# Moving three groups of loads in a hybrid decoder step on one Trainium2 core: y ahead of its tile's products, a block ring of four places, one decode state block per token

## The chip, the cores and the metric

The kernel runs on one core of a Trainium2 chip. A core has TensorE (PE in the profile, its weight loads PEld), VectorE (DVE), ScalarE (ACT), GpSimd (POOL) and SyncE (SP). In this kernel SP issues almost all loads and POOL almost all stores; SPq and POOLq are the queues from which they do so, and a DMA instruction whose buffer isn't free yet holds up everything behind it in its queue. The metric is the device time of one launch in microseconds (us), lower is better. Before the change three runs gave a median of 926.04 us (925.16 to 929.1).

## The reference

One layer of a decoder step with two groups of heads, in fp32, for one prompt of 1024 tokens (width 1024) and for 8 decode sequences of one new token each:

```python
hn = rmsnorm(x, g_norm)
u = hn @ w_in                          # 1024 x (1024 x 8200)
xa, za, uq, uk, uv, uo, zb, ui, uf = jnp.split(u, SPLIT_IDX, axis=-1)
yA, hA, bufA = rglru_branch(xa, ...)   # causal convolution of 4, gates, linear scan
hB, C, n, m = mlstm_seq(q, k, v, ...)  # 4 heads of 256, chunks of 128 tokens
yB = rmsnorm_per_head(sigmoid(uo) * hB) * g_mhead
merged = concatenate([yA * silu(za), yB * silu(zb)])
x = x + merged @ w_out                 # (1024 x 2048) x 1024
y = rmsnorm(x, g_final)
```

In decoding each of 8 sequences and 4 heads has a state C of 256 x 256, which is scaled, gets the outer product of the new k and v added, is stored, and is multiplied by q. Outputs are y for the prompt and for the samples, and all states.

## The kernel before, in words

**Products.** A product of two fp32 matrices is made of three matmuls in fp32r (`mm3`, L64 to L68): high times high, high times low, low times high. So each operand is split into a high part (a cast on ACT, L72) and a low part (a subtraction on DVE, L73). The big products use Strassen's scheme in the Winograd form with seven products of blocks, Q_P1 to Q_P7.

**Stages.** (1) The prompt is normalised, turned and split (to about 75 us of the span). (2) The input projection runs over 14 units of 512 columns (`prep`, `product`, `evac`; raw weights arrive in `raw0` and `raw1`). In its shadow run the gates, the RG-LRU branch (`rg_half`), and from about 124 us to 540 us the 32 decode states. (3) From about 660 us the mLSTM chunks (`m_a`, `m_k`, `m_b`, `m_g`, `m_z`) run with, between their parts, first the 28 products of the RG-LRU half with `w_out` (`r_prod`, 12 matmuls of 512 columns each), and then for each tile c of 128 tokens the mLSTM half of the output projection (`out_part(c, half)`, two halves of 24 matmuls). `last_tile` makes the eighth tile.

**The order of the work.** The Python program says which piece comes after which: `pop_bg` takes side work from three queues between the projection's halves, and `fill(k)` (L1617) takes k pieces of `work` between the parts of an mLSTM step. The whole program is recorded first; the framework then plans each engine's instruction order with costs of its own, where an instruction that comes early in the program has precedence but later work can be pulled ahead when an engine would be idle. Each engine then works through its own order strictly. Buffers with one tag share a number of places; a tile gets a place when a former one is released.

**Decode states.** `decode_steps(h)` gives per head one step `first` and one `token(b)` per sequence. A token scales the block on ACT (L995), adds the outer product on DVE (L997), stores it from POOL (L999), and fetches the next row of v (L968). Blocks lie in the tag `Cb` with four places of 256 KB. After every second token `products` multiplies the last two blocks by q (L1016), which frees their places. At an even token two blocks are fetched, i + 2 and i + 3 (L974).

**The ring.** The 28 operand blocks of the RG-LRU products (256 KB each) come from HBM into a ring of eight places: four in `raw1`, opened by the last `prep` (`r_open(0)`, L298), and four in `big` place 5, opened at product 1 (`r_open(1)`, L1438), when the split weights of Q_P3 have been made from that place. `r_op(n)` (L1422) splits block n into one of the six places of tag `ws` and fetches block n + 8 into the place that it has read; `r_prod(n)` calls `r_op(n + 2)`. When the ring is done, place 5 becomes `zb0` (L1323).

**The tail of a tile.** The sum of x and the RG-LRU half is accumulated in HBM in `d_p[c]` (L1430). `out_part(c, 0)` multiplies eight k-blocks, then allocates the two `y` tiles and loads them (L1576 to L1578), and adds the product (L1579). After the second half the tile's mean square is ready and `tail()` scales and stores it (L1533, L1534). `y`, the copies `zr` of the decode output (L1356, written by ACT at L1357), `zd`, `yd`, the norm gain `gf` and the copies `r` of the RG-LRU products all lie in the tag `stg` with seven places.

Of the kernel before, what the change touches and what calls it, by code (L numbers as in the profile page):

```python
# [9 lines left out]
F32 = mybir.dt.float32  # L10
# [7 lines left out]
P = 128  # L18
T = 1024
HT = 512  # L20
# [31 lines left out]
def hymba_kernel(  # L52
# [8 lines left out]
    ld = nc.sync.dma_start  # L61
# [28 lines left out]
    rawp = ctx.enter_context(tc.tile_pool(name="rawp", bufs=1))  # L90
# [10 lines left out]
    def sg(shape, name, dt=F32):  # L101

        return stg.tile(shape, dt, tag="stg", name=name)
# [63 lines left out]
    d_p = [[dram.tile([P, HT], F32, name=f"d_p{c}{a}") for a in range(2)] for c in range(NCH)]  # L167
# [111 lines left out]
    def prep(u, q):  # L279
        if q == Q_P5:  # L280
            dec_unit(u)
            V.tensor_tensor(blk(u, 0, 0), blk(u, 0, 0), blk(u, 1, 0), op=ALU.subtract)
            V.tensor_tensor(blk(u, 1, 0), blk(u, 1, 0), blk(u, 1, 1), op=ALU.add)
        if q == Q_P6:
            V.tensor_tensor(blk(u, 1, 0), blk(u, 1, 1), blk(u, 0, 0), op=ALU.subtract)
        src = {Q_P1: (0, 0), Q_P2: (0, 1), Q_P5: (1, 0), Q_P6: (1, 0), Q_P7: (0, 0), Q_P3: (0, 1), Q_P4: (1, 1)}
        hi, lo = ws([P, 4, 256], f"wh{u}_{q}"), ws([P, 4, 256], f"wl{u}_{q}")
        split(hi, lo, blk(u, *src[q]))
        wops[u, q] = hi, lo
        if q == Q_P6:  # L290
            V.tensor_tensor(blk(u, 0, 1), blk(u, 0, 1), blk(u, 1, 0), op=ALU.subtract)
        b = {Q_P7: 0, Q_P4: 1}.get(q)
        if b is not None:
            if u + 1 < len(units):
                load_raw(u + 1, b)
            else:
                if b == 1:
                    r_open(0)  # L298

    px = {}  # L300

# [668 lines left out]
    def fetch_C(i):  # L970
        if i < NB * NH:
            h, b = i // NB, i % NB
            ds_["C", i] = t = fpr["p"].tile([P, 2, 256], F32, tag="Cb", name="Cb", bufs=4)
            ld(t, st_C[0, b, h].rearrange("(kb p) v -> p kb v", p=P))  # L974

    def decode_steps(h):

        p2 = fpr["p"]
        qsel, qfirst, selq = fpr["qsel"], fpr["qfirst"], fpr["selq"]
        st = {}  # L980

        def first():
            st["kw"] = kw = p2.tile([P, 2, NB], F32, tag="kw", name="kw")
            V.tensor_tensor(kw, dk[:, 2 * h:2 * h + 2, :], dW[:, :, h].unsqueeze(1).to_broadcast([P, 2, NB]), op=ALU.mult)
            V.tensor_copy(qsel.rearrange("p k (m r) -> p k m r", r=9)[:, :, :, 0:5:4],
                          dq[:, 2 * h:2 * h + 2, :].rearrange("p k (m r) -> p k m r", r=2))
            V.tensor_copy(qfirst[:, :, :, 0], dq[:, 2 * h:2 * h + 2, 0:2])
            fetch_v(h, 0)

        def token(b):  # L990
            i = h * NB + b

            def f():
                vb_, C = ds_.pop(("v", i)), ds_["C", i]
                A.mul(C, C, dGI[:, b, h:h + 1])  # L995
                for kb in range(2):
                    V.scalar_tensor_tensor(C[:, kb, :], vb_, st["kw"][:, kb, b:b + 1], C[:, kb, :],  # L997
                                           op0=ALU.mult, op1=ALU.add)
                stq(s_C[0, b, h].rearrange("(kb p) v -> p kb v", p=P), C)  # L999
                if b + 1 < NB:  # L1000
                    fetch_v(h, b + 1)
                if b % 2:
                    late.append(lambda: late.append(products))
                else:
                    fetch_C(i + 2)
                    fetch_C(i + 3)


            def products():
                if b == 1:  # L1010
                    st["pq"] = ps("qp", [P, 512])
                pq = st["pq"]
                for g in range(4):
                    bb, kb = b - 1 + g // 2, g % 2
                    q, n = (qfirst[:, kb, bb, :], 32) if b == 1 else (qsel[:, kb, 4 * bb:4 * bb + 4], 4)
                    TE.matmul(pq[32 * g:32 * g + n, 0:256], q, ds_["C", h * NB + bb][:, kb, :], start=b == 1,  # L1016
                              stop=b == NB - 1, skip_group_check=True)
                for bb in (b - 1, b):
                    del ds_["C", h * NB + bb]
                if b == NB - 1:  # L1020
                    Z = sg([P, 256], "qC")
                    V.tensor_copy(Z, pq[:, 0:256])

                    def turn():
                        pt = pq[:, 256:272].rearrange("p (v b) -> p v b", v=2)
                        for vb in range(2):
                            TE.matmul(pt[:, vb, :], Z[:, vb * P:(vb + 1) * P], selq, start=True, stop=True)
                        V.tensor_copy(dqC[:, 2 * h:2 * h + 2, :], pt)
                    late.append(lambda: late.append(turn))
            return f  # L1030
        return [first] + [token(b) for b in range(NB)]
# [314 lines left out]
    def slot(n, name, dt=F32R):  # L1346
        if n < 0:
            return rawp.tile([P, 4, HT], dt, tag="raw0", name=name)
        return big(n, [P, 4, HT], name, dt)
# [53 lines left out]
    rring = []  # L1403
    rops = {}
    rx = {}

    def r_open(n):

        rring.append(rawp.tile([P, 4, HT], F32, tag="raw1", name="ring0") if n == 0 else slot(5, "ring1", F32))
        for i in range(4):  # L1410
            r_fetch(4 * n + i)

    def r_slot(n):
        return rring[n % 8 // 4][:, n % 4, :]

    def r_fetch(n):

        if n < NR:
            p, q = n // 7, RQ[n % 7]
            ld(r_slot(n), d_ro[q][:, p].rearrange("p k t -> p (k t)"))  # L1420

    def r_op(n):  # L1422

        if n < NR:
            rops[n] = o = ws([P, 2, HT], f"ro{n}")
            split(o[:, 0], o[:, 1], r_slot(n))
            r_fetch(n + 8)

    def put(c, a, t):
        stq(d_p[c][a], t, accum_op=ALU.add)  # L1430
# [1 line left out]
    def r_prod(n):  # L1432

        p, q = n // 7, RQ[n % 7]
        if n < 2:
            w_step((Q_P4, Q_P3)[n])
        if n == 1:
            r_open(1)  # L1438
        r_op(n + 2)
        o = rops.pop(n)  # L1440
        oh, ol = (o[:, i].rearrange("p (k t) -> p k t", k=4) for i in range(2))
        wh, wl = wr[q]
        if q == Q_P1:
            rx["X"] = ps("o", [P, 512])
        if q in (Q_P2, Q_P5):
            rx["Y"] = ps("o", [P, 512])
        X, Y = rx["X"], rx.get("Y")
        out = X if q in (Q_P1, Q_P6, Q_P7, Q_P4) else Y
        for k in range(4):
            mm3(out, oh[:, k, :], ol[:, k, :], wh[:, k, :], wl[:, k, :], q in (Q_P1, Q_P2, Q_P5) and k == 0,  # L1450
                q in (Q_P2, Q_P4, Q_P3) and k == 3)
            if k % 2:
                yield
        c = 4 * (p // 2) + p % 2
        if q in (Q_P1, Q_P5, Q_P6, Q_P4):
            rx[q] = t = sg([P, HT], f"r{q}")
            A.copy(t, Y if q == Q_P5 else X)
            if q == Q_P4:
                put(c, 1, t)
        else:  # L1460
            t = rx.pop({Q_P2: Q_P1, Q_P7: Q_P5, Q_P3: Q_P6}[q])
            V.tensor_tensor(t, t, X if q == Q_P7 else Y, op=ALU.add)
            put(c if q == Q_P2 else c + 2, q == Q_P7, t)
        r_after(n - (NR - 7))
# [92 lines left out]
    ot = {}  # L1557

    def out_part(c, half):

        if half == 0:
            ot[c] = {}
        elif c + 1 < NZ:
            z_split(c + 1)
        x = ot[c]
        x["p", half] = ps("o", [P, 512])
        mh, ml = ch[c]["mh"], ch[c]["ml"]
        hs = slice(half * HT, (half + 1) * HT)
        for k in range(8):
            w = wo[8 + k]  # L1570
            mm3(x["p", half], mh[:, k, :], ml[:, k, :], w[:, 0, hs], w[:, 1, hs], k == 0, k == 7)
            if k % 2:
                yield
        if half == 0:
            x["ms"] = fms()
            x["y"] = [sg([P, HT], f"y{n}") for n in range(2)]  # L1576
            for n in range(2):
                ld(x["y"][n], d_p[c][n])  # L1578
        V.tensor_tensor(x["y"][half], x["y"][half], x["p", half], op=ALU.add)  # L1579
        A.activation(x["p", half], x["y"][half], AF.Square, accum_out=x["ms"][:, half:half + 1])  # L1580
        if half == 1:
            finish(P, x["y"], x["ms"], y_p[0, c * P:(c + 1) * P, :], True)
            del ot[c], ch[c]
# [130 lines left out]
    for n in range(4, N):  # L1714
        c, h = n // 4, n % 4
# [90 lines left out]
```

## Time and profile before

| what | value |
|---|---|
| median of three runs (lowest, highest) | 926.04 us (925.16, 929.1) |
| the profiled execution's own time | 923.33 us |
| its span, first to last instruction | 921.6 us |
| granted TensorE clock | 0.998 |
| ACT busy, POOL busy | 591.1 us (64%), 192.0 us (21%) |
| DMA, mean over the span | 182 GB/s, 167.87 MB |

How to read it: a group line gives engine, operation and tiles as "out<-in", the count, the busy time, and the idle time of the engine just before such instructions with what ended it. A line of a chain is start, length, and the instruction or the transfer that everything later waited on. A line of waits is the waiting instruction, what it waited for, the total, the number of times, and the longest. In a timeline the bracket at the end is the engine's idle time ahead of that instruction and what ended it. All times are us from the span's start. One step of the page's 40 slices is 23.04 us.

### The profile page before, as it was taken

The numbers are of one execution on the slowest core, as the hardware profiler recorded it, in microseconds if no ns is written. First come the engines' busy times: TensorE is split into PE (matmuls) and PEld (weight loads), VectorE is DVE, ScalarE is ACT, GpSimd is POOL, SyncE is SP. The second block draws the span as 40 slices with busy tenths as digits, with TensorE's granted clock in tenths as the row PEclk, the third lists the DMA queues.
The fourth block names the chain that finished last, engine by engine and source line by source line (L and its number), as shares of the span: only waits on it lengthen the run. The fifth ranks groups of instructions, "written<-read, shape, count | busy, mean of one in ns | idle before, by whom it ended". The sixth has DMA issues, their size and how long they took to land.

```text
span 921.6 us, 15527 instructions
## 1 busy us (share of the span) xinstructions
PE 905.0 (98%) x5261; PEld 749.3 (81%) x5261; DVE 741.6 (80%) x1535; ACT 591.1 (64%) x1085; POOL 192.0 (21%) x317
## 2 busy tenths in 40 slices
PE   8999999999999999999999999999999999999997
PEld 6897777877687988787789898877778888778886
DVE  6874778888689878789888876679998779878873
ACT  7663456867667776576758775446876668656642
POOL 1111113112312222324333324010111110110120
PEclk9999999999999999999999999999999999999999
DMA  6611467456646566557765646436589798755642
GB/s 201 192 61 45 137 178 241 143 179 200 230 134 206 173 196 195 183 157 249 236 216 170 242 145 234 119 119 231 178 239 253 200 259 260 191 154 153 198 103 86
DMA packets 130600, 167.87 MB, mean 182 GB/s; under 512 B 17620, under 2 KB 98580, under 8 KB 130514
## 3 DMA queue, kind: packets, MB, share of 16 engines
q1 hardware_dynamic: 108934, 103.94, 37.4%
q0 software_dynamic: 21584, 62.95, 21.3%
q8 instruction: 41, 0.67, 0.3%
q14 instruction: 37, 0.30, 0.1%
q10 hardware_dynamic: 4, 0.00, 0.0%
HBM read 108.19 MB, written 62.92 MB: 186 GB/s over the span
## 4 chain that ended last, share of the span: by engine, by line
PE 88%; DVE 4%; ACT 3%; DMA 3%; issue 2%; POOL 0%; SPq 0%; DVEq 0%; ACTq 0%; POOLq 0%
PE ps_o L66 14%; PE ps_o L68 14%; PE ps_o L67 14%; PE ps_kv L66 10%; PE ps_kv L67 10%; PE ps_kv L68 10%; PE ps_tr L257 3%; PE ps_s L1198 2%; DMA Cb<-in_state_mlstm_C_dram 1%; DVE wl L73 1%; PE ps_qp L66 1%; PE ps_qp L67 1%; PE ps_qp L1016 1%; PE ps_qp L68 1%; PE ps_s L1200 1%
## 5 line engine op out<-in xcount | busy, mean ns | idle before, releaser
L72 ACT CAST wh<-raw 128x1024 fp32r<-128x1024 f32 x91 | 95.3, 1049 | 73.9 <-PE ps_o L67 27.7
L73 DVE TENSOR_TENSOR wl<-raw,wh 128x1024 fp32r<-128x1024 f32 x91 | 111.0, 1220 | 33.1 <-ACT wh L72 17.7
L66 PE MATMUL ps_kv<-cb_hi,wh 128*128 128x512 f32 x320 | 127.5, 398 | 0.0
L68 PE MATMUL ps_kv<-cb_hi,wl 128*128 128x512 f32 x320 | 125.3, 392 | 0.0
L67 PE MATMUL ps_kv<-cb_lo,wh 128*128 128x512 f32 x320 | 125.2, 391 | 0.0
L66 PE MATMUL ps_o<-cb_hi,wh 128*128 128x512 f32 x240 | 94.6, 394 | 0.0
L68 PE MATMUL ps_o<-cb_hi,wl 128*128 128x512 f32 x240 | 93.7, 390 | 0.0
L67 PE MATMUL ps_o<-cb_lo,wh 128*128 128x512 f32 x240 | 93.5, 390 | 0.0
L66 PEld LDWEIGHTS ps_kv<-cb_hi,wh 128*128 128x128 f32 x320 | 60.1, 188 | 21.4 <-issue 5.5
L67 PEld LDWEIGHTS ps_kv<-cb_lo,wh 128*128 128x128 f32 x320 | 60.2, 188 | 13.4 <-issue 1.7
L68 PEld LDWEIGHTS ps_kv<-cb_hi,wl 128*128 128x128 f32 x320 | 60.1, 188 | 12.9
L66 PE MATMUL ps_kv<-wh,cb_hi 128*128 128x256 f32 x192 | 55.3, 288 | 0.0
L67 PE MATMUL ps_kv<-wl,cb_hi 128*128 128x256 f32 x192 | 54.4, 283 | 0.0
L68 PE MATMUL ps_kv<-wh,cb_lo 128*128 128x256 f32 x192 | 54.3, 283 | 0.0
L66 PEld LDWEIGHTS ps_o<-cb_hi,wh 128*128 128x128 f32 x240 | 45.1, 188 | 10.0 <-issue 0.8
L66 PE MATMUL ps_o<-wo,mh 128*128 128x512 f32 (+1 forms) x136 | 53.1, 390 | 0.0
L68 PEld LDWEIGHTS ps_o<-cb_hi,wl 128*128 128x128 f32 x240 | 45.0, 188 | 9.8
L67 PEld LDWEIGHTS ps_o<-cb_lo,wh 128*128 128x128 f32 x240 | 45.1, 188 | 9.1
L68 PE MATMUL ps_o<-wo,ml 128*128 128x512 f32 (+1 forms) x136 | 51.7, 380 | 0.0
L67 PE MATMUL ps_o<-wo,mh 128*128 128x512 f32 (+1 forms) x136 | 51.5, 378 | 0.0
L66 PE MATMUL ps_o<-wh,cb_hi 128*128 128x256 f32 x144 | 40.9, 284 | 0.0
L67 PE MATMUL ps_o<-wl,cb_hi 128*128 128x256 f32 x144 | 40.7, 283 | 0.0
(550 smaller groups left out, 2601.6 us busy)
## 6 DMA issues: line engine op xcount, KB each, us to landing
raw<-in_w_in_dram SPq DMA_DIRECT2D x55, 512.0 KB
Cb<-in_state_mlstm_C_dram SPq DMA_DIRECT2D x32, 256.0 KB
out_dram<-Cb POOLq DMA_DIRECT2D x32, 256.0 KB, 4.7
qk<-d_qk SPq DMA_DIRECT2D x32, 256.0 KB
ring<-d_ro SPq DMA_DIRECT2D x28, 256.0 KB
d_qk<-s POOLq DMA_DIRECT2D x24, 256.0 KB, 4.5
d_x<-s POOLq DMA_DIRECT2D x16, 256.0 KB, 3.1
zsr<-d_y SPq DMA_DIRECT2D x16, 256.0 KB
```

The source lines that it names most:

```text
L66: TE.matmul(out, ah, bh, start=first, stop=False, skip_group_check=True)
L67: TE.matmul(out, ah, bl, start=False, stop=False, skip_group_check=True)
L68: TE.matmul(out, al, bh, start=False, stop=last, skip_group_check=True)
L72: a = A.copy(hi, src)
L73: V.tensor_tensor(lo, src, hi.bitcast(F32), op=ALU.subtract)
L257: TE.matmul(pz[32 * g:32 * g + 32, :], hnd[:, NB * k:NB * k + 32], raws[u, k // 4][:, k % 4, :], start=k < 4, stop=k >= 4, skip_group_chec ...
L1016: TE.matmul(pq[32 * g:32 * g + n, 0:256], q, ds_["C", h * NB + bb][:, kb, :], start=b == 1, stop=b == NB - 1, skip_group_check=True)
L1198: TE.matmul(S, qk[:, 2 + kb, :], qk[:, kb, :], start=kb == 0, stop=kb == 1)
L1200: TE.transpose(kn[:, kb * P:(kb + 1) * P], qk[:, 2 + kb, :], idF)
```

## The change

Three edits, with no change to what is computed.

```diff
@@ prep: the ring is opened by the last unit @@
-                    r_open(0)
+                    r_open()
@@ token(b) in decode_steps @@
                 if b % 2:
                     late.append(lambda: late.append(products))
-                else:
-                    fetch_C(i + 2)
-                    fetch_C(i + 3)
+                fetch_C(i + 2)
@@ the ring @@
-    def r_open(n):
-        rring.append(rawp.tile([P, 4, HT], F32, tag="raw1", name="ring0") if n == 0 else slot(5, "ring1", F32))
+    def r_open():
+        rring.append(rawp.tile([P, 4, HT], F32, tag="raw1", name="ring"))
         for i in range(4):
-            r_fetch(4 * n + i)
+            r_fetch(i)
     def r_slot(n):
-        return rring[n % 8 // 4][:, n % 4, :]
+        return rring[0][:, n % 4, :]
@@ r_op @@
             split(o[:, 0], o[:, 1], r_slot(n))
-            r_fetch(n + 8)
+            r_fetch(n + 4)
@@ r_prod @@
-        if n == 1:
-            r_open(1)
         r_op(n + 2)
@@ out_part @@
         if half == 0:
-            ot[c] = {}
+            ot[c] = {"y": [sg([P, HT], f"y{n}") for n in range(2)]}
+            for n in range(2):
+                ld(ot[c]["y"][n], d_p[c][n])
...
         if half == 0:
             x["ms"] = fms()
-            x["y"] = [sg([P, HT], f"y{n}") for n in range(2)]
-            for n in range(2):
-                ld(x["y"][n], d_p[c][n])
```

The `y` tiles of a tile of tokens take their places and are loaded ahead of the tile's first product, in the program's order, where they were loaded after the eighth k-block. The ring has the four places in `raw1` alone, and a block is fetched when the block four before it has been split; the four loads of `r_open(1)` are gone as such, the number of block loads stays 28. A token fetches block i + 2 alone, so that of each pair the second block's fetch stands one token later in the program. `last_tile`, which loads its own `y`, is not changed.

## The prediction

> **What bounds the kernel now.** I read the page first, then the chain in order of time, then what PE waited for, since only PE's waits can be turned into time here.
>
> ```profile
> PE 905.0 (98%) x5261; PEld 749.3 (81%) x5261; DVE 741.6 (80%) x1535; ACT 591.1 (64%) x1085; POOL 192.0 (21%) x317
> PE 88%; DVE 4%; ACT 3%; DMA 3%; issue 2%; POOL 0%; SPq 0%; DVEq 0%; ACTq 0%; POOLq 0%
> ```
>
> PE is busy for 905.0 of 921.6 us, and the chain that ended last runs over PE for 88%. DMA has 3% of it. In order of time that is three transfers, one for each edit:
>
> ```profile
> 456.47 8.91 DMA Cb<-in_state_mlstm_C_dram
> 673.25 3.81 DMA ring<-d_ro
> 807.81 5.17 DMA y<-d_p
> ```
>
> It would be wrong to add these up to 17.9 us: while a transfer is on the chain, PE may work on something else. The waits of PE say what was lost:
>
> ```profile
> PE ps_qp L1303 <- ACT hh L1254: 2.3, 1, 2.3
> PE ps_o L66 <- ACT ro L72: 1.4, 1, 1.4
> PE ps_tr L257 <- ACT ig L777: 1.4, 1, 1.4
> PE ps_tr L265 <- ACT Z L260: 0.6, 2, 0.3
> PEld ps_qp L1303 <- ACT hh L1254: 2.7, 1, 2.7
> PEld ps_o L66 <- ACT ro L72: 1.6, 1, 1.6
> ```
>
> The first four are of PE's ten rows of waits, among them the three longest; the last two are the weight loads' waits for the same two things. Each is traced back below. The windows tell how little else there is to win:
>
> ```profile
> 100.00:540.00 440.00, 437.83 (x2492) 356.14 (x2491) 368.52 (x653) 298.04 (x429) 121.58 (x194) 1.00 0.60 193
> 660.00:790.00 130.00, 128.57 (x728) 111.12 (x728) 113.73 (x274) 92.66 (x219) 20.36 (x28) 1.00 0.86 238
> 790.00:880.00 90.00, 87.73 (x516) 72.17 (x515) 74.36 (x228) 53.69 (x163) 11.15 (x18) 1.00 0.57 165
> ```
>
> The second column is PE's busy time. In the decode stage (100 to 540) it lacks 2.2 us, in the ring's stage (660 to 790) 1.4 us, in the tiles' stage up to 880 2.3 us: 5.9 us in all where the edits act.
>
> **The ring.** Reading the timeline from 658 to 678:
>
> ```profile
> 658.82 2.12 SPq L1420 DMA_DIRECT2D ring<-d_ro  x2
> 666.81 8.19 SPq L1420 DMA_DIRECT2D ring<-d_ro  x6
> 673.25 1.74 SPq L1420 DMA_DIRECT2D ring<-d_ro  x4
> 677.09 0.62 ACT L72 CAST ro<-ring 128x512 fp32r<-128x512 f32 x1 [0.90 <-DMA ring<-d_ro]
> 677.76 0.50 PE L66 MATMUL ps_o<-wr4h,ro 128*128 128x512 f32 x1 [1.42 <-ACT ro L72]
> ```
>
> The two loads at 658.82 and 660.6 are blocks 8 and 9, fetched as blocks 0 and 1 have been split. Of the six from 666.81 on, the last four, at 673.25, are `r_open(1)`: blocks 4 to 7. Block 4 is the operand of the fifth product, whose first matmul uses `wr4h`; the cast waits for its landing, 3.8 us after the issue, and PE waits 1.42 us for the cast. With the change the loads at 658.82 and 660.6 are blocks 4 and 5, those at 666.8 and 670.5 blocks 6 and 7. At 3.8 us each they land at about 662.6, 664.4, 670.6 and 674.3, block 4 some 13 us before its product. So the 1.4 us go. What is late next at that place? The weights:
>
> ```profile
> 663.17 2.35 DVE L73 TENSOR_TENSOR wr4l<-ws,wr4h 128x1024 fp32r<-128x1024 f32 x2
> ```
>
> They end at 665.5, so nothing. Four loads leave SP's queue here, at 0.44 us each of issue; 28 block loads stay 28 in all. From then on, is four products ahead enough?
>
> ```profile
> L66 PE MATMUL ps_o<-wr0h,ro x16: 387/389/475, 660.7 to 751.2; 128*128 128x512 f32 x16
> L72 ACT CAST ro<-ring x28: 602/618/626, 649.8 to 752.6; 128x512 fp32r<-128x512 f32 x28
> SPq L1420 <- DVE ro L73: 17.8, 7, 11.2
> ```
>
> `wr0h` serves products 0, 7, 14 and 21: 22 products in 90.8 us, 4.1 us each, so four are 16.5 us. The turn of a place is SP's wait for the split (longest 11.2 us, in the crowded opening) and the transfer of 3.8 us: 15.0 us at worst. The last cast begins at 752.6, when product 21 has just ended: casts run up to six products ahead, by the six places of `ws`, and that margin of 25 us comes on top. The SP wait is not added: the fetch of block n + 8 stood behind the same split and in the same queue. I take **-1.4 us**; bounds are -1.6 (the weight load's wait for the same cast) and, if the ring runs short, the first rival.
>
> **The y loads.** The timeline from 807 to 817:
>
> ```profile
> 807.61 0.57 ACT L1357 COPY zr<-ps_tr 128x512 f32<-128x512 f32 x1
> 807.81 0.86 SPq L1578 DMA_DIRECT2D y<-d_p  x2
> 813.08 0.69 DVE L1579 TENSOR_TENSOR y<-y,ps_o 128x512 f32<-128x512 f32 x1 [5.72 <-DMA y<-d_p]
> 813.80 0.60 ACT L1580 ACTIVATE ps_o<-y 128x512 f32<-128x512 f32 x1 [5.62 <-DVE y L1579]
> 816.29 0.66 PE L1303 MATMUL ps_qp<-idF,hh 128*128 128x128 f32 x4 [2.27 <-ACT hh L1254]
> ```
>
> This is tile 1. DVE stands 5.72 us on the load, ACT 5.62 us behind DVE, and the read of `ps_qp` at L1254 stands behind L1580 on ACT; the transposes at L1303 need that bank, and PE loses 2.27 us. Why so late? The load follows the second `zr` copy by 0.2 us, and in the program the `zr` tile of `wo_dec` 12 to 15 is asked for just before tile 1's y. Places of `stg` seem to be granted in the order in which they are asked for. With the edit y of tile 1 is asked for at the end of tile 0's second half, ahead of that `zr` and behind the first one:
>
> ```profile
> 793.63 0.59 ACT L1357 COPY zr<-ps_tr 128x512 f32<-128x512 f32 x1 [0.63 <-PE ps_tr L1481]
> 792.98 0.38 SPq L1165 DMA_DIRECT2D so<-d_so  x1
> 798.91 0.32 SPq L1147 DMA_DIRECT2D vt<-d_v  x1
> ```
>
> SP issues nothing between 793.4 and 798.9, so the two loads (0.86 us of SP's time) fit there and push nothing back; at 5.2 us they land at about 799 to 800, 13 us early. Seven places hold `gf` 2, y of tile 0 2, `zr` 1 and y of tile 1 2: full, but not over. The second `zr` needs the first one's place, whose store goes out here:
>
> ```profile
> 794.51 0.83 POOL L1358 DMA_DIRECT2D d_z<-zr  x1 [8.81 <-ACT zr L1357]
> DMA to landing us min/median/max: 3.6/4.1/6.5
> ```
>
> At most 6.5 us, so by 801, against 807.6. What is late next: without its 5.62 us of waiting ACT comes to L1254 right behind that bank's matmuls, and the transposes find it read. I take **-2.3 us**, bounds -2.7 (the weight load's wait) and 0. The other tiles are not helped: their loads go out when a place is freed, whatever the program's order. Tile 6 shows it; its first y goes out as the second of the pair at 864.44, 32 us ahead of its use:
>
> ```profile
> 864.44 0.91 SPq L1578 DMA_DIRECT2D y<-d_p  x2
> 897.62 0.69 DVE L1579 TENSOR_TENSOR y<-y,ps_o 128x512 f32<-128x512 f32 x1 [0.51 <-PE ps_o L68]
> ```
>
> **The state blocks.** The same 32 loads on the same queue, the odd ones one token later in the program. What they cost now:
>
> ```profile
> ACT Cb L995 <- DMA Cb<-in_state_mlstm_C_dram: 20.8, 13, 3.5
> 248.26 0.73 ACT L995 ACTIVATE Cb<-Cb,dGI 128x512 f32<-128x512 f32 x1 [1.95 <-DMA Cb<-in_state_mlstm_C_dram]
> 251.07 1.49 PE L257 MATMUL ps_tr<-raw,hnd 128*32 128x512 f32 x12 [1.40 <-ACT ig L777]
> 507.68 0.72 ACT L995 ACTIVATE Cb<-Cb,dGI 128x512 f32<-128x512 f32 x1 [3.49 <-DMA Cb<-in_state_mlstm_C_dram]
> 508.72 0.72 ACT L995 ACTIVATE Cb<-Cb,dGI 128x512 f32<-128x512 f32 x1 [0.32 <-DMA Cb<-in_state_mlstm_C_dram]
> ```
>
> ACT stands 20.8 us on these blocks; PE loses 1.4 us to it once (at 251, through the gates' casts queued behind), and part of the 0.6 us at L265, shortly after the transfer that the chain shows at 456.47. Does a block fetched alone land sooner? At 507.68 and 508.72 the two of a pair land 1.04 us apart, so the second is served after the first and takes little from it: the wait for the first, which is the one that hurts, stays. A rule of the Trainium skill speaks to this, DMA: Bandwidth & Descriptors, section "Queues, rings and completion order": on each DMA engine descriptors of one queue are consumed in ring order, though without a guarantee of finishing in that order; by it this edit wins nothing at 251, and these two rows agree. Can the odd block now come too late? It is fetched two tokens ahead, as the even one is. If every odd block made ACT wait as the even ones do, the 20.8 us would double, and PE lost 1.4 to 2.0 us to them: +2.0 at most by these rows. I take **0**, bounds -2.0 and +2.0.
>
> **The sum.** -1.4 - 2.3 + 0 = -3.7 us. The profiled execution took 923.33 us (span 921.6), the median of the runs is 2.7 us above it; applied to the median, 926.04 - 3.7 = **922.3 us**. The Trainium skill, Perfetto Trace Analysis, section "Identifying the Most-Contended Engine", says that busy time of matmuls is a bad measure of PE's headroom and weight-load busy time a good one. By PEld the two waits are 1.6 and 2.7 us, and the time would be 921.7; the 0.6 us lie within the range.
>
> **The rivals.** (1) *The ring runs short*, the case that ends slower: the turn of a place exceeds four products (16.5 us against 15.0 at worst), the cast stands in ACT's queue ahead of the mLSTM's casts, and PE waits as it did at 677.76, once in each of the six rounds of four. For it speaks a crowded stage (DMA share 0.86, 660 to 790), against it the casts' lead. Price 6 x 1.4 = 8.4, less 1.4 and 2.3: 926.04 + 4.7 = 930.7. (2) *The y load doesn't move*: if places are granted otherwise than I read it, tile 1's y still goes out at 807.8, or the second `zr` waits for its place and takes the gain back: 926.04 - 1.4 = 924.6. (3) *The state blocks help after all*: with one load less in flight the 1.4 us at L257 and the 0.6 us at L265 go: 922.3 - 2.0 = 920.3. (4) *The planner's order shifts*: from the first state block on, work that can go in any order may be put differently and meet new short waits. Price: what PE lacks in the decode stage once more, 2.2 us: 924.5.
>
> **How the numbers follow.** Forecast 922.3 (own range 921 to 924) 0.44; (1) 0.12, (2) 0.13, (3) 0.20, (4) 0.11. The range runs from 918.5 (rival 3, less the 0.6 us of PEld and the 0.9 us by which the lowest run lies under the median) to 928 (rivals 2 and 4 plus the 3.1 us of the highest run); rival 1 is left out. A measurement of this kernel can tell about 0.5% from no change, 4.6 us. Faster by more is below 921.4: rival 3 and three tenths of the forecast, 0.33. Slower by more is above 930.7: most of rival 1, 0.10. Between: 0.57.
>
> **What would show it.** Ring: no PE wait on ACT `ro`, block loads in ones and twos from 658 to 675, no six in a row. y: tile 1's loads near 794, no DVE wait on y, no 2.3 us at L1303. State blocks: the ACT row stays near 20 us. Wrong would be: rows "ACT ro <- DMA ring" of several us, a new wait of ACT on a place for `zr`, or PE idle in 100 to 540 clearly off 2.2 us.

## The result, and the profile after

The changed kernel takes **929.74 us** (median of 20 runs, 927.47 to 933.91), the kernel before 925.84 us in the same comparison (20 runs, 921.9 to 929.1): ratio 1.0051, 95% interval 1.0039 to 1.0062. It is slower, where 922.3 us and a range of 918.5 to 928.0 had been forecast. The profiled execution took 927.47 us, its span is 925.7 us, 4.1 us more than before.

First the page of the changed kernel, its busy times, the chain by engine and the longest wait of PE:

```profile
PE 908.8 (98%) x5261; PEld 752.2 (81%) x5261; DVE 741.8 (80%) x1535; ACT 591.1 (64%) x1085; POOL 191.9 (21%) x317
PE 82%; DVE 7%; ACT 4%; DMA 4%; issue 2%; SPq 1%; POOL 0%; DVEq 0%; POOLq 0%; ACTq 0%
PE ps_o L66 <- ACT r L1453: 3.1, 4, 1.7
```

The waits at L1303 and on ACT `ro` have gone from PE's list; a wait on ACT's copies `r` has come. A trap lies in the first line: PE's *busy* time grew by 3.8 us (905.0 before) for the same 5261 matmuls. Nearly the whole loss is booked as busy, so whoever looks only at idle time does not find it. What finds it is the start of the same instruction in both traces. Compared so, the changed kernel is 0.1 us ahead at 660 us of the time before, 5.25 us behind at 720, 7.0 behind at 750, and 4.5 behind from 820 on. By stage (columns as before: PE's busy time second, then the weight loads, DVE, ACT, POOL, the granted clock, the DMA share and GB/s):

```profile
100.00:540.00 440.00, 438.01 (x2492) 356.39 (x2491) 368.86 (x652) 298.10 (x429) 121.48 (x194) 1.00 0.60 193
660.00:790.00 130.00, 125.06 (x688) 106.56 (x687) 106.44 (x258) 88.67 (x208) 18.94 (x26) 0.99 0.81 226
790.00:880.00 90.00, 90.00 (x532) 74.66 (x531) 76.85 (x230) 55.28 (x167) 11.14 (x18) 1.00 0.63 179
```

The decode stage is as it was (437.83 before), the tiles' stage has lost its gap (87.73 before, 90.00 now), and the ring's stage has opened one: 728 matmuls fell into it before, 688 now. One row measures it, that of the first weights, products 0, 7, 14 and 21; it lasted from 660.7 to 751.2 before:

```profile
L66 PE MATMUL ps_o<-wr0h,ro x16: 387/390/476, 660.7 to 758.3; 128*128 128x512 f32 x16
```

That is 97.6 us instead of 90.5: **the ring costs 7.1 us**. The waits of 655 to 800 say where:

```profile
ACT ro L72 <- DMA ring<-d_ro: 10.5, 7, 5.2
DVE ro L73 <- ACT ro L72: 10.5, 5, 4.4
PEld ps_o L66 <- ACT r L1453: 4.0, 4, 1.9
```

ACT, with its casts, waits 10.5 us for block loads, where it waited 0.9 us before. The timeline shows the longest of these waits and what followed (ACT; DVE's low part of block 9; SP issues block 13; ACT; PE):

```profile
683.76 0.62 ACT L72 CAST ro<-ring 128x512 fp32r<-128x512 f32 x1 [2.23 <-DMA ring<-d_ro]
691.80 0.68 DVE L73 TENSOR_TENSOR ro<-ring,ro 128x512 fp32r<-128x512 f32 x1
692.86 0.62 SPq L1418 DMA_DIRECT2D ring<-d_ro  x1
701.74 0.62 ACT L72 CAST ro<-ring 128x512 fp32r<-128x512 f32 x1 [5.16 <-DMA ring<-d_ro]
702.57 0.62 ACT L72 CAST Ch<-Cf 128x516 fp32r<-128x516 f32 x1
704.44 0.47 ACT L1204 ACTIVATE kh<-ps_s,de_t 128x256 fp32r<-128x256 f32 x1
706.52 0.39 PE L68 MATMUL ps_kv<-vh,kl 128*128 128x258 f32 x1 [0.60 <-DVE kl L1206]
711.89 0.39 PE L67 MATMUL ps_qp<-Cl,qh 128*128 128x258 f32 x1 [0.53 <-DVE Cl L73]
713.04 0.50 PE L66 MATMUL ps_o<-wr4h,ro 128*128 128x512 f32 x1 [0.40 <-ACT r L1453]
721.30 0.48 PE L66 MATMUL ps_o<-wr5h,ro 128*128 128x512 f32 x1
```

The cast at 683.76 is block 9's, the one at 701.74 is that of block 13, which went into block 9's place. The place took 18.0 us to turn: 9.1 to the fetch, 8.9 from there to the landing. Of the 9.1, 8.0 are DVE's order: the place is free when DVE has made the low part from it, and that begins at 691.80. (For blocks 4 to 10 it begins 8.0 to 13.3 us after the cast.) Block 13 is the operand of product 13, and that begins at 721.30 (its weights are `wr5h`): PE did not need the cast for another 19 us. But the cast stood where it stood in ACT's order, and behind it stood `Ch`, `kh` and the copies `r`, which PE did need. So PE never waited for `ro`; it waited for the work behind that cast.

### The profile page after: what moved, and what is told of

Its sections match the earlier page's. It is cut to its first block, busy times and chain, and to the rows that moved or that the text cites. A ratio compares the mean times of both kernels' runs of the same rounds, so it can differ in the third digit from the quotient of the medians.

```text
span 925.7 us, 15517 instructions
## 1 busy us (share of the span) xinstructions
PE 908.8 (98%) x5261; PEld 752.2 (81%) x5261; DVE 741.8 (80%) x1535; ACT 591.1 (64%) x1085; POOL 191.9 (21%) x317
## 4 chain that ended last, share of the span: by engine, by line
PE 82%; DVE 7%; ACT 4%; DMA 4%; issue 2%; SPq 1%; POOL 0%; DVEq 0%; POOLq 0%; ACTq 0%
PE ps_o L66 13%; PE ps_o L68 13%; PE ps_o L67 13%; PE ps_kv L66 10%; PE ps_kv L67 9%; PE ps_kv L68 9%; PE ps_tr L257 3%; DMA ring<-d_ro 2%; PE ps_s L1196 1%; DVE wl L73 1%; PE ps_qp L1014 1%; PE ps_tr L827 1%; PE ps_s L827 1%; PE ps_tr L265 1%; PE ps_qp L66 1%
## 5 line engine op out<-in xcount | busy, mean ns | idle before, releaser
L73 DVE TENSOR_TENSOR wl<-raw,wh 128x1024 fp32r<-128x1024 f32 x91 | 111.1, 1221 | 33.1 <-ACT wh L72 17.9
L68 PE MATMUL ps_o<-wh,cb_lo 128*128 128x256 f32 x144 | 40.8, 283 | 0.0
```

The costliest lines, as they stand in the source:

```text
L68: TE.matmul(out, al, bh, start=False, stop=last, skip_group_check=True)
L73: V.tensor_tensor(lo, src, hi.bitcast(F32), op=ALU.subtract)
```

## The experiments

Each kernel was timed beside the kernel before on the same chip (whose median there was 924.89 to 925.84 us), and the ratio is to that. The number that tells the ring's cost is the distance from the first to the last matmul in the row of `wr0h` (products 0 to 21) in each profile. All of them together:

| kernel | places | median us | ratio to before, 95% | row of `wr0h`, us | ACT's waits on block loads, 655 to 800, us |
|---|---|---|---|---|---|
| before | 8 | 925.84 | | 90.5 | 0.9 |
| changed | 4 | 929.74 | 1.0051 [1.0039, 1.0062] | 97.6 | 10.5 |
| ring's edit alone | 4 | 930.78 | 1.0055 [1.0037, 1.0073] | 96.6 | 13.2 |
| y's edit alone | 8 | 922.88 | 0.9970 [0.9958, 0.9983] | 90.3 | 0.7 |
| state blocks alone | 8 | 924.87 | 0.9997 [0.9983, 1.0012] | 89.9 | 0.4 |
| changed, casts held | 4 | 924.57 | 0.9995 [0.9983, 1.0007] | 90.3 | none |
| changed, place 5 kept | 4 | 927.99 | 1.0045 [1.0028, 1.0063] | 96.4 | 12.2 |
| ring of six | 6 | 928.76 | 1.0034 [1.0008, 1.0061] | 91.9 and 93.4 | 2.4 and 2.4 |
| eight, other opening, y | 8 | 923.31 | 0.9982 [0.9971, 0.9993] | 92.0 | 3.8 |
| changed, casts held to 23 | 4 | 927.29 | 1.0029 [1.0015, 1.0043] | 90.4 | 6.4 |
| changed, three operand places | 4 | 924.39 | 1.0006 [0.9990, 1.0021] | 90.5 | none |
| ring of five | 5 | 927.57 | 1.0042 [1.0026, 1.0057] | 95.9 | 7.7 |
| eight, other opening, held, y | 8 | 922.11 | 0.9971 [0.9956, 0.9985] | 90.1 | none |

Three theories stood against each other. **T1**: the planner places the casts far ahead of their products; with four places they wait there for their landing, and ACT's fixed order passes the wait on. **T2**: the free place 5 lets the loads of `zb0` go out early, and SP, held up by them, is late with the ring's last blocks. **T3**: four places are too few in whatever order.

### One edit at a time

The ring alone (the other two edits undone in the changed kernel):

> Only the ring's edit: one ring of four blocks, refetched four products ahead; the y loads and the state blocks as before. The theory (T1: casts stand early in ACT's fixed order and wait there for block landings of 5 to 9 us): all of the loss is the ring's, about +7.0 us against before, 932 to 934, with ACT's waits on the ring at about 10 us in 655 to 800 where before had 0.9, PE's waits for the r copies at about 3 us, and a granted clock under 0.9 somewhere in 695 to 715. As the prediction had it (four products ahead are enough): -1.4 us, 924.4. If instead the loss comes of the three edits together (the y loads, asked for earlier, taking SP's queue): 924 to 928 here.

The y loads alone, in the kernel before:

```diff
-            ot[c] = {}
+            ot[c] = {"y": [sg([P, HT], f"y{n}") for n in range(2)]}
+            for n in range(2):
+                ld(ot[c]["y"][n], d_p[c][n])
...
-            x["y"] = [sg([P, HT], f"y{n}") for n in range(2)]
-            for n in range(2):
-                ld(x["y"][n], d_p[c][n])
```

> Only the y loads' edit. The prediction's step: -2.3 us, so about 923.5, no PE wait at the transposes of hh into ps_qp, tile 1's two y loads near 794. T1 says the same, since it puts the loss wholly on the ring. If y's loads are what crowds the ring's last loads: 926 or above, with waits of ACT on block operands 20 to 27.

The state blocks alone, in the kernel before:

> Only the state blocks' edit: the odd block is fetched one token later. Prediction and T1: 0, so 925 to 926.5, PE's busy time in 100 to 540 within 0.5 us of 437.8, ACT's wait on Cb near 20 us. Rival (one load fewer in flight helps): -1.4 to -2.0, 924. Rival (one load later hurts): +1.4 to +2.0, 928.

Measured: 930.78, 922.88 and 924.87 us beside 925.11 us before: +5.7, -2.2 and -0.2 us, 3.2 together before rounding; the change as a whole makes +3.9. The rows of the ring alone:

```profile
L66 PE MATMUL ps_o<-wr0h,ro x16: 387/389/477, 662.2 to 758.8; 128*128 128x512 f32 x16
ACT ro L72 <- DMA ring<-d_ro: 13.2, 9, 4.2
```

The ring's +5.7 lies a little under the 7 that the trace of the changed kernel shows and was expected here, and 930.78 under the expected 932 to 934; the granted clock, expected under 0.9 somewhere in 695 to 715, was 1.00 there. The edits hardly touch each other: all of the loss is the ring's, and y's step was right. In the kernel with state blocks alone PE is busy for 435.96 us in 100 to 540, which is 1.9 less than expected; but the kernel with y alone, whose decode stage is that of before, has 435.86, so this difference is one between executions and not the edit's.

### The casts held back

In the changed kernel each cast from block 3 on is put, with its low part, behind the last `r` copy on ACT and the last `r` addition on DVE:

```diff
-            split(o[:, 0], o[:, 1], r_slot(n))
+            with ExitStack() as es:
+                for k in ("A", "V"):
+                    if k in rx:
+                        es.enter_context(tc.issue_after(rx[k].ins))
+                split(o[:, 0], o[:, 1], r_slot(n))
...
-            A.copy(t, Y if q == Q_P5 else X)
+            rx["A"] = A.copy(t, Y if q == Q_P5 else X)
...
-            V.tensor_tensor(t, t, X if q == Q_P7 else Y, op=ALU.add)
+            rx["V"] = V.tensor_tensor(t, t, X if q == Q_P7 else Y, op=ALU.add)
```

> The changed kernel, but each block's cast and its low part are put behind the last r copy and the last r add in ACT's and DVE's order, so that the planner cannot place them further ahead than that. T1 (the order is at fault: casts placed up to 20 us before their product wait for a landing and hold up what stands behind them): the waits of ACT on the ring fall from 10 us to under 3, the time to 922 to 925. T3 (four places are too few whatever the order): 929 or more, with PE's waits moved from the r copies to the casts themselves. A third outcome: the casts now stand so late that PE waits at each of the 28 products, 0.3 us or more each: 932 or above.

Measured: 924.57 us, in the expected stretch. The rows of its ring: the 27 casts from 655 us on, the row of `wr0h`, and a new wait of ACT:

```profile
L72 ACT CAST ro<-ring x27: 602/622/633, 655.9 to 772.0; 128x512 fp32r<-128x512 f32 x27
L66 PE MATMUL ps_o<-wr0h,ro x16: 389/393/475, 663.9 to 754.2; 128*128 128x512 f32 x16
ACT wo L1491 <- DMA oraw<-in_w_out_dram: 2.5, 1, 2.5
```

No cast waits for a block any more, with the same four places, the same loads and the same transfers, and the row lasts 90.3 us, as before. T1 holds, and T3 falls for the products that the row covers: there four places are enough when the casts keep pace with the products. (The hold also brings the low parts close behind: those of blocks 8 to 10 begin 0.7 to 0.9 us after their casts. How much is owed to the casts standing later and how much to the places coming free sooner, these runs don't tell apart; both are the order.) It isn't the 922.9 of the kernel with y alone, though. Behind product 21 it loses 2.2 us: there ACT waits 2.5 us for the first block of output weights, and the last casts stand behind that. The changed kernel loses nothing there. Why this one does stays open: the next experiment was to tell, and doesn't.

The same with blocks 24 to 27 left free (`if k in rx and n < 24`):

> As the kernel with the held casts, but blocks 24 to 27 are left free: there the hold put two casts behind an r copy that itself stood behind a 2.5 us wait for weights, and PE lost 2.0 us at 768 to 776. T1: those 2.0 us come back, ring's stage about -0.1 to -1 against before, 922.3 to 923. If the 2.0 us come of four places and not of the hold: 924.5 as it was.

Measured: 927.29 us: worse, against every expectation, T1's too. What the trace shows fits T1 all the same. ACT's timeline, from the last held casts on:

```profile
748.12 1.67 ACT L72 CAST ro<-ring 128x512 fp32r<-128x512 f32 x3
753.27 0.62 ACT L72 CAST ro<-ring 128x512 fp32r<-128x512 f32 x1 [1.47 <-DMA ring<-d_ro]
759.69 0.62 ACT L72 CAST ro<-ring 128x512 fp32r<-128x512 f32 x1 [4.92 <-DMA ring<-d_ro]
761.05 0.47 ACT L1252 ACTIVATE hh<-ps_qp,gi_t 128x257 f32<-128x257 f32 x1
```

The free casts stand further forward: 24 and 25 run in one go with 23 at 748.12 (with all casts held, 25 began at 756.1), and 26 and 27 then wait for their places to be filled. PE waits 2.1 us for the `hh` behind the last one and is 5.8 us further behind at 770 (past the last product that the row of `wr0h` counts). The stall of 700 to 720 has moved to the one place where the order was free. (That the planner puts a cast where, by its own costs, the block has landed is an inference; its costs aren't in the trace.)

### Fewer places for the split blocks

The lead can also be taken away without laying down an order: a split block needs a place of `ws`, and three of the six are kept occupied.

```diff
+        if n == 2:
+            rx["keep"] = [ws([P, 2, HT], f"keep{i}", F32) for i in range(3)]
+            for t in rx["keep"]:
+                V.memset(t[:, 0, 0:1], 0.0)
         r_op(n + 2)
+        if n == 25:
+            for t in rx.pop("keep"):
+                V.tensor_copy(t[:, 0, 1:2], rops[27][:, 0, 0:1].bitcast(F32))
```

> The changed kernel, with three of the six places of ws kept occupied from product 2 to product 25 (six copies or fills of one column), so that at most three split blocks can stand at once: the planner cannot place a cast more than some three products ahead. No order is laid down by hand. T1 (the lead of the casts, which the planner builds up over the six places of ws, is what makes ACT wait for landings): as with the held casts, 922.5 to 925, ACT's waits on the ring under 2 us in 680 to 760. If the held casts helped by something else (the order laid down by hand changes the whole plan): 929 or more, with the waits as in the changed kernel.

Measured: 924.39 us. The 26 casts and the row of `wr0h`:

```profile
L72 ACT CAST ro<-ring x26: 609/622/636, 656.4 to 770.3; 128x512 fp32r<-128x512 f32 x26
L66 PE MATMUL ps_o<-wr0h,ro x16: 389/393/475, 661.8 to 752.3; 128*128 128x512 f32 x16
```

Again no cast waits for a block and the row lasts 90.5 us. So it is the lead, and not something that the laid-down order does besides; here too the low parts of blocks 8 to 10 follow their casts by 0.7 to 1.0 us. *Less* buffering behind the casts repaired the loss of buffering ahead of them. Here, too, some 2.6 us are lost behind product 21, where ACT waits 2.8 us for the output weights.

### Place 5 kept occupied

T2 had rows of its own in the changed kernel: SP's issue of the ring stops at 715.61 and goes on at 727.00, behind a load of `zb0`, and the cast of block 21 and the copy `r` that follow are late (SP; ACT; PE). The cast's wait is put down to a matmul; the experiment speaks for the late block:

```profile
715.61 0.32 SPq L1418 DMA_DIRECT2D ring<-d_ro  x1
723.57 0.32 SPq L1324 DMA_DIRECT2D zb<-d_mz  x1
727.00 2.38 SPq L1418 DMA_DIRECT2D ring<-d_ro  x3
735.41 0.62 ACT L72 CAST ro<-ring 128x512 fp32r<-128x512 f32 x1 [2.89 <-PE ps_tr L68]
742.67 0.50 PE L66 MATMUL ps_o<-wr4h,ro 128*128 128x512 f32 x1 [1.73 <-ACT r L1453]
```

The experiment puts a tile into place 5 and lets go of it at product 21:

```diff
+        if n == 1:
+            rx["hold"] = slot(5, "hold", F32)
+            V.memset(rx["hold"][:, 0, 0:1], 0.0)
         r_op(n + 2)
+        if n == 21:
+            V.tensor_copy(rx["hold"][:, 0, 1:2], rops[23][:, 0, 0:1].bitcast(F32))
```

> The changed kernel, with place 5 of big kept occupied up to product 21 (by a tile that nothing but two copies of one column touches), so that the zb0 load stays as late as before. T2 (the zb0 loads, which the free place lets go out at 716, hold SP up 7.6 us and so the ring's last fetches): 1.8 to 2.0 us of the 7 come back, time about 927.7, no wait of ACT on block 21, and the stall of 1.7 us at the r copy near 735 gone. T1 (casts wait for landings whatever SP does later): the 5.2 us at 700 to 720 stay, with ACT's waits on blocks 9, 11 and 13; 929.7 if T2 is nothing.

Measured: 927.99 us, ratio 1.0045 against 1.0051 for the changed kernel, with overlapping intervals. The stall at 742 is gone, as T2 said: block 21 is fetched 3.7 us earlier, at 723.31, and its cast waits for nothing. But the trace loses 1.7 us at 760 to 772 instead, where ACT waits for the output weights. T2 explains 1.8 us at that place and no more; the 5 us at 700 to 720 stay. The time itself can't tell the two kernels apart.

### How many places the order needs

In the kernel before the planner let twelve casts (blocks 4 to 15) run between 677.1 and 702.6, which is one in 2.3 us, though the products take 4.1 us each:

```profile
L72 ACT CAST ro<-ring x12: 603/617/621, 677.1 to 702.6; 128x512 fp32r<-128x512 f32 x12
```

Four casts at that pace take 9.3 us, five 11.6, six 13.9, eight 18.5. A place turned in 18.0 us. By this rough estimate five and six should run short, and eight should just do. Six places, in the changed kernel (with five, 1, 5 and 5 stand for 2, 6 and 6):

```diff
-        for i in range(4):
-            r_fetch(i)
+        for i in range(2 if n else 4):
+            r_fetch(4 * n + i)
...
-        return rring[0][:, n % 4, :]
+        return rring[n % 6 // 4][:, n % 6 % 4, :]
...
-            r_fetch(n + 4)
+            r_fetch(n + 6)
```

(`r_open(n)` opens the second part in place 5 at product 1, as in the kernel before.)

> The y and state block edits as in the changed kernel, the ring with six places (four in raw1, two in place 5, opened at product 1) and fetched six products ahead; the planner's order is not touched. The prediction's step said that four ahead are enough; T1 says that the casts stand up to 20 us, five products, ahead of their product, so that six are barely enough: ACT's waits on the ring fall from 10.5 us to 1 to 3, the ring's loss from +7 to between 0 and +2, time 922.5 to 925. If the loss comes of something that six places share with four (an order that the planner changes as soon as the ring is not eight): 927 or more.

> As the ring of six, with one place fewer, fetched five products ahead. In the kernels of before and of eight places the casts of blocks 4 to 15 come every 2 us, so five casts take some 10.5 us against a turn (issue, landing, cast, low part) of 8 to 13 us in the crowded stretch. T1: between the two, ring's loss +2 to +6, ACT's waits on the ring 4 to 9 us, time 925 to 929. If the turn is to be held against products (4.1 us each, 20 us for five), as the prediction held it: no loss, 922.9.

> The ring of six once more, for a second profile, since its times ran from 922.8 to 934.9 while its first profile (923.8) showed no loss in the ring's stage. T1 with little to spare: where a landing takes a few us longer than in the first profile, ACT waits for it on the ring and PE behind it, in 680 to 720; a time above 927 goes with ACT's waits on the ring of over 5 us. If the spread is of the clock and not of the ring: a time above 927 with the waits as they were (2.4 us) and a lower granted clock.

The waits of ACT on the block loads, 655 to 800: ring of six, ring of five, ring of six in a second execution, each with the row of `wr0h` ahead of it:

```profile
L66 PE MATMUL ps_o<-wr0h,ro x16: 387/389/475, 661.4 to 753.3; 128*128 128x512 f32 x16
ACT ro L72 <- DMA ring<-d_ro: 2.4, 2, 2.0
```

```profile
L66 PE MATMUL ps_o<-wr0h,ro x16: 387/389/475, 661.0 to 756.9; 128*128 128x512 f32 x16
ACT ro L72 <- DMA ring<-d_ro: 7.7, 4, 3.9
```

```profile
L66 PE MATMUL ps_o<-wr0h,ro x16: 387/389/475, 661.0 to 754.4; 128*128 128x512 f32 x16
ACT ro L72 <- DMA ring<-d_ro: 2.4, 2, 2.2
```

With eight, six, five and four places the row lasts 90.5, 91.9 to 93.4, 95.9 and 97.6 us, and ACT waits 0.9, 2.4, 7.7 and 10.5 us: the ring's loss grows with each place taken away. Held against products, five places should have cost nothing. The medians of the whole kernel don't show the order (928.76 us with six, 927.57 with five): five came as expected, six missed its 922.5 to 925.

For the ring of six something stays open. Eleven of its twelve runs lie between 922.8 and 934.9 us; the two profiled executions, 923.8 and 927.3 us, differ by 1.5 us in the ring's stage at the same waits (the clock, below) and by 1.7 us at 895, where a load of `so` came late and DVE waited 3.3 us for it instead of 1.6. Why other runs came to over 930 us, no profile shows. Their granted clocks, 0.993 to 0.995 against 0.996 to 0.999 in the six under 928 us, are a part of it: 0.004 of 930 us is 3.7 us by estimate, and the two groups lie 7.6 us apart in the mean. Of the last expectation the second alternative came nearer (over 927 us with the waits as they were and a lower clock), but the clock is only 1.5 us of it.

### A version that beats both

The kernel before with y's edit, and blocks 4, 5 and 6 fetched into the places of blocks 0, 1 and 2:

```diff
-            r_fetch(4 * n + i)
+            r_fetch(7 * n + i)
...
-        return rring[n % 8 // 4][:, n % 4, :]
+        n = n if n < 12 else 4 + (n - 4) % 8
+        k = n if n < 4 else (0, 1, 2, 4, 5, 6, 7, 3)[n - 4]
+        return rring[k // 4][:, k % 4, :]
...
-            r_fetch(n + 8)
+            r_fetch(n + (4 if n < 3 else 8))
```

> The kernel before with the y edit, and the ring of eight opened otherwise: blocks 4, 5 and 6 are fetched into the places that blocks 0, 1 and 2 leave, block 7 and three more into place 5 at product 1. It should have both of the gains that the prediction summed: -2.4 for y (923.4 before for e2's kernel: 922.9) and -1.0 to -1.4 for the wait on block 4, with the ring eight ahead afterwards: 921.4 to 922. If the opening's wait is only handed on to the next thing that is late there, as in the changed kernel: 922.9, as with y alone.

> The ring of eight with the other opening and the y edit, and the casts of blocks 3 to 11 put behind the last r copy. T1: the 3.6 us by which ACT waited there for block 7, and PE's 2 us behind it, go; so does the wait for block 4: 921.5 to 922, a little under y alone. If the opening has no gain to give, since whatever stands there is late (weights of the first products): 922.9 or more.

The first takes 923.31 us: it gains nothing on y alone (922.88). PE's wait on `ro` is gone, but the casts of the opening run earlier, and now block 7's cast waits (ACT), with `hh` behind it and PE behind that:

```profile
682.08 0.62 ACT L72 CAST ro<-ring 128x512 fp32r<-128x512 f32 x1 [3.57 <-DMA ring<-d_ro]
682.61 0.47 ACT L1254 ACTIVATE hh<-ps_qp,gi_t 128x257 f32<-128x257 f32 x1
683.13 0.66 PE L1303 MATMUL ps_qp<-idF,hh 128*128 128x128 f32 x4 [1.84 <-ACT hh L1254]
```

It is T1 in small, and against the first alternative of the expectation. The second puts the casts of blocks 3 to 11 behind the last `r` copy and `r` addition, as above (`n < 12`); the wait goes, and it takes **922.11 us**, ratio 0.9971. That is faster than both kernels, but not to be told apart from y alone (0.9970). A gain of the opening isn't shown: its row of `wr0h` lasts 90.1 us, and with the opening as before that row lasts 89.9 to 90.5 us in the three profiles of eight places.

## Why the prediction was wrong

**The ring: wrong, and it decided.** The step that failed is the answer to "is four products ahead enough?": 15.0 us for the turn of a place against 16.5 us for four products, with the casts' lead as a "margin of 25 us on top". Both halves fail.

- The turn was held against products, but a place is freed by its *split* (cast and low part) and needed by a *cast*. ACT's order was there to be read in the trace of before: twelve casts at 2.3 us each. Four of them make 9.3 us.
- The lead is no reserve. It has to be built up, and the casts that build it up are those that run at 2.3 us. Once an instruction has its place in a fixed order, that PE could do without its result for another 19 us helps nobody behind it. The two experiments that took the lead away took the waits away.
- The turn was too small as well: 18.0 us where 15.0 was called the worst. The landing was taken at 3.8 us, from the one block that anybody had waited for; block 13 landed 8.9 us after its issue. And DVE began block 9's low part, which frees the place, 8.0 us after the cast.

The mechanism itself stood in the prediction as rival 1, with its chain (the cast ahead of the mLSTM's casts in ACT's queue) and 930.7 us, against 929.74 measured. It got 0.12 because "the casts' lead" was counted against it. Its price was made otherwise than it came: not 1.4 us in each of six rounds on `ro`, but 5.2 us in one stretch where the lead was built up and 1.8 us at 742. That its 930.7 lies so near is luck: 8.4 us stood for 7.1, and 1.4 us were taken off for an opening that gave nothing. One of the signs that the prediction named, no wait of PE on ACT `ro`, came true in a kernel that got slower; the other one, waits of ACT on the ring of several us, was the one to watch.

**The opening: half right.** The wait on `ro` at 677.76 went, as predicted, with its four loads spread. But waits of 0.6 and 0.3 us on the copies `r` came in its place, and the trace stands level there. "What is late next?" was asked of the weights only, and not of ACT's other work, which the earlier casts push back.

**y: right.** -2.3 us predicted; 2.5 us in the trace at 813, -2.2 us by the median of y alone. Tile 1's loads go out at 800.48 in the changed kernel, which is 7.0 us behind there, so at 793.5 on the old scale (predicted: near 794), and DVE waits for them no more:

```profile
800.48 0.84 SPq L1560 DMA_DIRECT2D y<-d_p  x2
812.74 0.68 DVE L1574 TENSOR_TENSOR y<-y,ps_o 128x512 f32<-128x512 f32 x1
```

**The state blocks: right.** 0 predicted, -0.2 us measured (0.9983 to 1.0012). ACT's wait on the blocks is 17.9 us with this edit alone and 23.5 us in the changed kernel, but 16.6 and 17.6 us in the two kernels without the edit that were profiled beside it (20.8 before), so executions differ by as much. By the rule that was cited there (the Trainium skill, DMA: Bandwidth & Descriptors, "Queues, rings and completion order") nothing was to be won, and the measurement agrees.

**The sum.** -1.4 - 2.3 + 0 had to read +7.1 - 2.5 + 0 with the opening included in the first term: +4.6 us; half a us came back elsewhere, and the spans differ by 4.1. The range left out rival 1 on purpose, and that was the case that came. (Its lower end, by the terms given, comes to 918.8 and not 918.5; nothing hangs on it.)

## What to carry to other kernels

Before shortening a prefetch, compare the turn of a place (release, issue, landing in the crowded stretch) with the shortest time in which the *consumer's instruction stream* runs through as many places, and not with the mean rate of the final product. A consumer that runs far ahead in a strictly ordered queue doesn't make a late load harmless; it makes everything behind it wait, for data that nobody needs yet. When a ring must be small, limit the lead too: fewer places behind the consumer, or an order that ties it to the product.

## What the runs showed of the hardware

PE's granted clock dips to half after short stalls, and nearly the same stall does it in one execution and not in the other. The ring of six twice, 4 us each, from 686 on, right behind a wait of PE of 1.75 us in the first and 1.96 us in the second:

```profile
686.00:690.00 4.00, 4.00 (x25) 3.60 (x26) 4.00 (x12) 2.19 (x7) 0.88 (x1) 1.00 0.75 226
```

```profile
686.00:690.00 4.00, 4.00 (x18) 3.59 (x17) 2.89 (x9) 0.97 (x4) 0.88 (x1) 0.58 0.79 211
```

PE counts as fully busy in both, with 25 matmuls counted in one and 18 in the other; 4 us at 0.58 cost 1.7 us, by estimate from the clock. In the changed kernel the same happens behind gaps of 0.6 us and less:

```profile
706.00:708.00 2.00, 1.48 (x8) 1.48 (x9) 2.00 (x9) 0.84 (x5) 0.57 (x1) 0.77 0.62 190
708.00:710.00 2.00, 2.00 (x6) 1.51 (x6) 1.29 (x5) 1.97 (x7) 0.27 (x1) 0.50 0.22 40
710.00:712.00 2.00, 1.47 (x10) 1.17 (x8) 1.93 (x7) 2.00 (x6) 0.00 (x0) 0.87 0.93 214
```

That is again 1.7 us of its 5.2 (2 us at 0.77, 0.50 and 0.87); in both cases it comes to some 3.4 us at half speed. It isn't the cause of them: the kernel with the ring alone loses 6.1 us in the row of `wr0h` (96.6 against 90.5) at a mean clock of 1.00 in 660 to 790. The Trainium skill, TensorE: Matmul & The Clock Gate, section "Part 1: The HAM clock gate (the "warmup" mystery)", has the clock at half after an idle window of some 3.4 us. These runs agree on the half, but not on the idleness: PE had pauses of 2 us and under, and single gaps of 0.6 us, when it came.
